# A PEER decoder trunk on one core: the low-part products of a dense tile go last, and the second products alternate between two halves

## The chip, the core and the metric

The kernel runs on one core of one Trainium2 chip. The metric is device time in microseconds (us). Three runs of the kernel before took 3287.05, 3287.91 and 3290.01 us, a median of 3287.91.

## What is computed

The reference is a decoder trunk of two layers on 512 tokens of width 1024. Layer 0 mixes tokens by retention, layer 1 by differential attention. Each is followed by a layer norm, a PEER feed-forward block and another layer norm. The change lies in the PEER block, where each token picks 128 of 16384 experts:

```python
def peer_ffn(x, w_q, subkeys, u, v):
    ...
        top, pos = lax.top_k(cand, PEER_TOPK)
        idx = jnp.take_along_axis(cidx, pos, axis=-1).reshape(PEER_CHUNK, PEER_HEADS * PEER_TOPK)
        gate = jax.nn.softmax(top, axis=-1).reshape(PEER_CHUNK, PEER_HEADS * PEER_TOPK)
        u_e = jnp.take(u, idx, axis=0)
        v_e = jnp.take(v, idx, axis=0)
        act = jax.nn.gelu(jnp.einsum('ted,td->te', u_e, xc).astype(jnp.float32))
        return jnp.einsum('te,ted->td', (gate * act).astype(v_e.dtype), v_e)
```

## The kernel before

Products of float32 matrices are made of three products. Each operand is split into a high part, rounded by ScalarE (`split`, line 103), and a low part, the rest, by VectorE or GpSimd (line 104). `mm3` (line 106) adds high x high, high x low and low x high into one PSUM bank. `wload` brings a 512 KB block of weights into one of nine raw buffers and splits it into `wh` and `wl`, which have three buffers each.

The first 128 tokens take the sparse way: their experts' rows are gathered one by one (`sparse_u`, `sparse_v`), a VectorE instruction for each. The other 384 tokens (`DT`) take the dense way: for all 16384 experts, 128 at a time, the activation is computed, multiplied by a gate that is zero for experts not picked, and used in a second product.

- A **dense tile** (`u_tile`, line 869) is the first product of 128 experts with 384 tokens: 8 blocks `k` of the width, three products of 128x384 each, 24 in all, into a bank `mu` or `rt`; ScalarE's gelu takes the result to `uact`.
- A **second-product step** (`v_mm`, line 888, called for 3 token tiles `t`) multiplies the gated activations (`wwh`, `wwl`, made by `v_prep`) with 128 rows of v, in two halves `c` of 512 columns: 18 products of 128x512 into six accumulators, four banks `pj` and two `rt`, which stay open over all 128 steps.

Names in a profile's rows are "out<-moving,stationary": `mu<-xth,wh` is high x high, `mu<-xtl,wh` the low part of x with the high part of the weights, `mu<-xth,wl` the product that needs `wl`. In the second products `wwh` and `wwl` are the stationary operand.

`peer` runs in two parts per layer. In the **first part** top-k, one-hot gates (`gates`, `gmat`) and sparse dot products run on VectorE, while TensorE makes the first 82 dense tiles ahead and stores them (`ad`). In the **second part** the 128 steps run; the stored tiles are read back for the first 82, after which dense tiles and steps take turns, with four tiles ahead (`LEAD`). The main line of that loop is

```python
preps.append(v_prep(kp, l, a, act, g[:, :, a % GA, :]))
if a < P - NB:
    for t in range(DT // P):
        v_mm(preps[0], t, acc)
```

Each engine runs its instructions in a fixed order. That order is made when the program is built, by a scheduler that places instructions by their operands' readiness in its own timeline; so an edit to the order of products can move instructions on other engines.

Of the kernel before, what the change touches and what calls it, by code (L numbers as in the profile page):

```python
# [29 lines left out]
P = 128  # L30
S = 512
D = 1024
TB = S // P
KD = D // P
# [10 lines left out]
DT = 384  # L45
# [18 lines left out]
def build(tc, I, out):  # L64
    nc = tc.nc
    ctx = ExitStack()
    with ctx:
# [18 lines left out]
        XTH = xp.tile([P, KD, S], F32R, name="xth")  # L86
        XTL = xp.tile([P, KD, S], F32R, name="xtl")

        def bank(tag):
            return psum.tile([P, 512], F32, name=tag, tag=tag, bufs=4 if tag == "pj" else 2)  # L90


        newest = {}
# [12 lines left out]
        def mm3(o, ah, al, bh, bl, start, stop):  # L106
            nc.tensor.matmul(o, ah, bh, start=start, stop=False)  # L107
            nc.tensor.matmul(o, ah, bl, start=False, stop=False)  # L108
            return nc.tensor.matmul(o, al, bh, start=False, stop=stop)  # L109

        def wload(src, eng=None, pool=None, tag="", bufs=3, dst=None):
            a = src.shape[1]
            pool = pool or wp
            raw = wp.tile([P, 1024], F32, name="wraw", tag="wraw", bufs=RING)
            nc.sync.dma_start(raw.rearrange("p (a b) -> p a b", a=a), src)
            if dst is None:
                h = pool.tile([P, 1024], F32R, name="wh", tag="wh" + tag, bufs=bufs)
                l = pool.tile([P, 1024], F32R, name="wl", tag="wl" + tag, bufs=bufs)
            else:
                h, l = dst  # L120
            split(h, l, raw, eng)
            return h.rearrange("p (a b) -> p a b", a=a), l.rearrange("p (a b) -> p a b", a=a)
# [746 lines left out]
        def u_tile(dp, l, a, tag="mu"):  # L869
            uh, ul = wload(I[f"ut{l}"][a])  # L870
            b = bank(tag)
            for k in range(KD):
                newest["mm"] = mm3(b[:, :DT], uh[:, k, :], ul[:, k, :], XTH[:, k, S - DT:], XTL[:, k, S - DT:], k == 0, k == KD - 1)
            act = dp.tile([P, DT], F32, name="uact", tag="uact", bufs=LEAD + 1)
            newest["gelu"] = nc.scalar.activation(act, b[:, :DT], AF.Gelu_apprx_tanh)
            return act
# [11 lines left out]
        def v_mm(prep, t, acc):  # L888
            a, (vh, vl), wh, wl = prep
            ts = slice(t * P, t * P + P)  # L890
            for c in range(2):
                mm3(acc[t][c], wh[:, ts], wl[:, ts], vh[:, c, :], vl[:, c, :], a == 0, a == P - 1)

        def peer(l, norm, feed, prepare):
            with tc.tile_pool(name="sp", bufs=1, reuse_waits="tile") as sp, tc.tile_pool(name="dp", bufs=1, reuse_waits="tile") as dp:
# [6 lines left out]
                with tc.tile_pool(name="p1", bufs=1, reuse_waits="tile") as kp:  # L902
# [10 lines left out]
                    with tc.tile_pool(name="tk", bufs=1, reuse_waits="tile") as tp:  # L913
# [43 lines left out]
                        for cost in gates():  # L957
                            tv += cost
                            while tu < tv and nu < P:
                                act = u_tile(dp, l, nu, ("mu", "rt")[nu % 2])  # L960
                                nc.sync.dma_start(ad[nu], act)
                                nu += 1
                                tu += UT
                                while nd < DOTS * (nu - LAG):
                                    with behind("low"):
                                        next(su, None)
                                    nd += 1
                                    tv += 1.2
                with tc.tile_pool(name="p2", bufs=1, reuse_waits="tile") as kp:
# [18 lines left out]
                    def u_ahead():  # L988
                        nonlocal used
                        while len(ahead) < LEAD and nu + used < P:  # L990
                            ahead.append(u_tile(dp, l, nu + used))
                            used += 1
# [3 lines left out]
                    for a in range(P):  # L996
                        if a < GA * NG0:
                            g = G0[a // GA]
                        elif a % GA == 0:
                            g = dp.tile([P, DT // GT, GA, GT], F32, name="gl", tag="gl", bufs=2)  # L1000
                            nc.sync.dma_start(g.rearrange("p q a t -> p (q a t)"),
                                              gd.rearrange("g p q f -> g p (q f)")[a // GA - NG0])
                        if a < nu:
                            act = kp.tile([P, DT], F32, name="aact", tag="aact", bufs=4)
                            nc.sync.dma_start(act, ad[a])
                        else:
                            act = ahead.pop(0)
                            u_ahead()
                        due += (flow * time[a] - load[a]) / row
# [4 lines that stand above are left out]
                            preps.pop()  # L1014
                        while done < due:
                            next(su2, None)
                            done += 1
# [5 lines left out]
                    for t in range(DT // P):  # L1023
                        for p in preps:
                            v_mm(p, t, acc)
                        if t and norm.dst is None:
                            norm.tr()
                        for c in range(2):
                            half_sum(acc[t][c], t + 1, c, True)
                        norm.ln(t + 1)  # L1030
# [74 lines left out]
```

## Time and profile before

| what | value |
|---|---|
| median of three runs | 3287.91 us |
| the profiled execution, its own time | 3291.58 us |
| its span, first to last instruction | 3289.8 us |
| mean granted TensorE clock | 0.989 of full speed |
| HBM traffic | 692.88 MB read, 78.38 MB written |

PE is TensorE's matmuls, PEld its weight loads, DVE is VectorE, ACT ScalarE, POOL GpSimd, SP the engine that issues most transfers. The page tells shares of the whole span. A table by windows gives each engine's busy time in a stretch with the granted clock, a list of waits gives who stood still for whom, and a timeline gives single instructions with, in brackets, the idle time before one and what ended it. Two matmul records overlap, as a matmul's row lasts past the next one's start; the step from start to start is the pace.

### The profile page before, as it was taken

How to read it: one execution, taken by the hardware profiler on the slowest of the kernel's cores; microseconds unless marked ns; L12 is line 12 of the kernel's file. 1: busy time of each engine (PE TensorE's matmuls, PEld its weight loads, DVE VectorE, ACT ScalarE, POOL GpSimd, SP SyncE). 2: the span in 40 equal slices, each digit the busy share in tenths (PEclk: the TensorE clock that was granted, in tenths of full speed). 3: DMA queues.
4: the chain of work that ended last, by engine and by line, in shares of the span. 5: the costliest groups of instructions: out<-in, count | busy, mean ns of one | idle time of the engine just before them, and what ended most of it. 6: DMA issues, size and time to landing. Idle time of an engine off the chain costs nothing.

```text
span 3289.8 us, 47157 instructions
## 1 busy us (share of the span) xinstructions
PE 3202.7 (97%) x16666; PEld 2844.6 (86%) x16666; DVE 2520.6 (77%) x4849; ACT 1397.4 (42%) x2436; POOL 1020.3 (31%) x663
## 2 busy tenths in 40 slices
PE   9999999899999999999999999989999999999998
PEld 7888889899998888889888668989999788888987
DVE  4444468999868888888863564899987888888886
ACT  3323333367763333333333652335777333333332
POOL 1101330211113333455424423125531233345540
PEclk9999999999999999999999999999999999999999
DMA  5222223577789999899943212347787999999993
GB/s 212 87 84 87 90 91 123 186 237 250 254 271 347 359 353 351 331 350 356 345 151 102 71 34 80 122 166 240 251 260 256 350 354 366 341 334 349 354 339 135
DMA packets 310078, 774.39 MB, mean 235 GB/s; under 512 B 25936, under 2 KB 154320, under 8 KB 306256
## 3 DMA queue, kind: packets, MB, share of 16 engines
q1 hardware_dynamic: 236112, 502.89, 43.5%
q0 software_dynamic: 73728, 268.47, 22.6%
q8 instruction: 131, 2.15, 0.3%
q14 instruction: 107, 0.88, 0.1%
HBM read 692.88 MB, written 78.38 MB: 234 GB/s over the span
## 4 chain that ended last, share of the span: by engine, by line
PE 60%; DVE 6%; issue 2%; ACT 1%; DMA 1%; POOL 0%; POOLq 0%; DVEq 0%; ACTq 0%
PE pj L107 9%; PE pj L108 9%; PE pj L109 9%; PE mu L109 5%; PE mu L107 5%; PE mu L108 5%; PE rt L108 5%; PE rt L107 5%; PE rt L109 5%; PE pj L844 2%; DVE wl L104 1%; PE mu L499 1%; DVE tk_idf L736 1%; DVE x L767 0%; PE rt L536 0%
## 5 line engine op out<-in xcount | busy, mean ns | idle before, releaser
L103 ACT ACTIVATE wh<-wraw 128x1024 fp32r<-128x1024 f32 x632 | 659.0, 1054 | 590.9 <-PE mu L108 119.6
L104 DVE TENSOR_TENSOR wl<-wraw,wh 128x1024 fp32r<-128x1024 f32 x572 | 699.2, 1232 | 202.1 <-ACT wh L103 193.9
L752 POOL DMA_INDIRECT ug<-in_u,idx x256 | 433.2, 1692 | 1155.9 <-DVE wl L104 577.6
L109 PE MATMUL mu<-xth,wl 128*128 128x384 f32 (+1 forms) x1424 | 481.5, 338 | 16.5 <-DVE wl L104 16.5
L107 PE MATMUL mu<-xth,wh 128*128 128x384 f32 (+1 forms) x1424 | 482.1, 339 | 9.8 <-ACT wh L103 7.3
L108 PE MATMUL mu<-xtl,wh 128*128 128x384 f32 (+1 forms) x1424 | 478.8, 336 | 0.0
L765 POOL DMA_INDIRECT vg<-in_v,idx x256 | 337.7, 1319 | 330.0 <-DVE x L767 233.0
L108 PE MATMUL pj<-wl,wwh 128*128 128x512 f32 x1024 | 400.6, 391 | 0.0
L103 ACT ACTIVATE wwh<-w 128x384 fp32r<-128x384 f32 x256 | 134.3, 526 | 625.6 <-issue 365.9
L109 PE MATMUL pj<-wh,wwl 128*128 128x512 f32 x1024 | 397.2, 389 | 0.0
L107 PE MATMUL pj<-wh,wwh 128*128 128x512 f32 x1024 | 382.5, 392 | 7.4 <-ACT wwh L103 7.4
L754 DVE CUSTOM_DVE_ANT_0 scr<-ug,x 128x1024 bf16<-128x1024 f32 x256 | 314.4, 1228 | 33.6 <-DMA ug<-in_u,idx 33.2
L767 DVE SCALAR_TENSOR_TENSOR x<-vg,wgt,x 128x1024 f32<-128x1024 f32 x256 | 328.5, 1283 | 3.9 <-DMA vg<-in_v,idx 0.4
L109 PEld LDWEIGHTS mu<-xth,wl 128*128 128x128 f32 x1424 | 270.2, 190 | 21.9 <-DVE wl L104 21.6
L107 PEld LDWEIGHTS mu<-xth,wh 128*128 128x128 f32 x1424 | 270.3, 190 | 16.4 <-ACT wh L103 9.6
L108 PEld LDWEIGHTS mu<-xtl,wh 128*128 128x128 f32 x1424 | 270.6, 190 | 3.6
L104 DVE TENSOR_TENSOR wwl<-w,wwh 128x384 fp32r<-128x384 f32 x256 | 143.0, 560 | 125.1 <-ACT wwh L103 112.6
L109 PE MATMUL rt<-xth,wl 128*128 128x384 f32 (+1 forms) x688 | 230.2, 335 | 7.2 <-DVE wl L104 7.2
L107 PE MATMUL rt<-xth,wh 128*128 128x384 f32 (+1 forms) x688 | 231.1, 336 | 0.2
L107 PEld LDWEIGHTS pj<-wh,wwh 128*128 128x128 f32 x1024 | 192.7, 189 | 44.5 <-ACT wwh L103 8.0
L108 PE MATMUL rt<-xtl,wh 128*128 128x384 f32 (+1 forms) x688 | 229.5, 334 | 0.5 <-DVE xtl L104 0.5
L109 PEld LDWEIGHTS pj<-wh,wwl 128*128 128x128 f32 x1024 | 192.3, 188 | 40.1
(242 smaller groups left out, 6316.2 us busy)
## 6 DMA issues: line engine op xcount, KB each, us to landing
wraw<-in_ut SPq DMA_DIRECT2D x256, 512.0 KB
wraw<-in_v SPq DMA_DIRECT2D x256, 512.0 KB
gd<-g_st SPq DMA_DIRECT2D x48, 896.0 KB
gl<-gd SPq DMA_DIRECT2D x28, 1536.0 KB
ad<-uact SPq DMA_DIRECT2D x164, 192.0 KB
aact<-ad SPq DMA_DIRECT2D x164, 192.0 KB
wraw<-in_w_in SPq DMA_DIRECT2D x48, 512.0 KB
wraw<-in_peer_w_q SPq DMA_DIRECT2D x32, 512.0 KB
```

Source lines behind the costliest of these rows:

```text
L103: nc.scalar.activation(h, src, AF.Copy)
L104: newest["low"] = (eng or nc.vector).tensor_tensor(out=l, in0=src, in1=h.bitcast(F32), op=OP.subtract)
L107: nc.tensor.matmul(o, ah, bh, start=start, stop=False)
L108: nc.tensor.matmul(o, ah, bl, start=False, stop=False)
L109: return nc.tensor.matmul(o, al, bh, start=False, stop=stop)
L499: nc.tensor.matmul(b[:, :n], qt[g][ms, h, qb * P:qb * P + P], kt[g][ms, h, :n], start=True, stop=True)
L736: nc.vector.reduce_sum(out=idf[:, hs, :], in_=ex.rearrange("p h c k -> p h k c"), axis=AX.X)
L752: nc.gpsimd.indirect_dma_start(out=u, out_offset=None, in_=I[f"u{l}"], in_offset=bass.IndirectOffsetOnAxis(ap=idx[:, j:j + 1], axis=0))
L754: nc.vector.tensor_tensor_reduce(out=scr, in0=u, in1=X[t], scale=1.0, scalar=0.0, op0=OP.mult, op1=OP.add, accum_out=act[:, j:j + 1])
L765: nc.gpsimd.indirect_dma_start(out=v, out_offset=None, in_=I[f"v{l}"], in_offset=bass.IndirectOffsetOnAxis(ap=idx[:, j:j + 1], axis=0))
L767: nc.vector.scalar_tensor_tensor(out=X[t], in0=v, scalar=w[:, j:j + 1], in1=X[t], op0=OP.mult, op1=OP.add)
L844: nc.tensor.matmul(b[:, i * P:i * P + P], oh[:, 1, i, :], oh[:, 0, i, :], start=True, stop=True)
```

## The change

In `u_tile` the 24 products come in another order: for each `k` the two with the high part `uh`, then for each `k` the one with the low part `ul`. In `v_mm` the loop over the kind of product is now the outer one and the loop over the two halves the inner one. The products and their operands are the same.

```diff
--- before.py
+++ after.py
@@ -869,8 +869,12 @@
         def u_tile(dp, l, a, tag="mu"):
             uh, ul = wload(I[f"ut{l}"][a])
             b = bank(tag)
+
             for k in range(KD):
-                newest["mm"] = mm3(b[:, :DT], uh[:, k, :], ul[:, k, :], XTH[:, k, S - DT:], XTL[:, k, S - DT:], k == 0, k == KD - 1)
+                nc.tensor.matmul(b[:, :DT], uh[:, k, :], XTH[:, k, S - DT:], start=k == 0, stop=False)
+                nc.tensor.matmul(b[:, :DT], uh[:, k, :], XTL[:, k, S - DT:], start=False, stop=False)
+            for k in range(KD):
+                newest["mm"] = nc.tensor.matmul(b[:, :DT], ul[:, k, :], XTH[:, k, S - DT:], start=False, stop=k == KD - 1)
             act = dp.tile([P, DT], F32, name="uact", tag="uact", bufs=LEAD + 1)
             newest["gelu"] = nc.scalar.activation(act, b[:, :DT], AF.Gelu_apprx_tanh)
             return act
@@ -888,8 +892,9 @@
         def v_mm(prep, t, acc):
             a, (vh, vl), wh, wl = prep
             ts = slice(t * P, t * P + P)
-            for c in range(2):
-                mm3(acc[t][c], wh[:, ts], wl[:, ts], vh[:, c, :], vl[:, c, :], a == 0, a == P - 1)
+            for i, (w, v) in enumerate(((wh, vh), (wh, vl), (wl, vh))):
+                for c in range(2):
+                    nc.tensor.matmul(acc[t][c], w[:, ts], v[:, c, :], start=a == 0 and i == 0, stop=a == P - 1 and i == 2)
 
         def peer(l, norm, feed, prepare):
             with tc.tile_pool(name="sp", bufs=1, reuse_waits="tile") as sp, tc.tile_pool(name="dp", bufs=1, reuse_waits="tile") as dp:
```

Since the scheduler sets the order, three places of the built program are shown before and now.

TensorE, first part of layer 0, tile `rt_4858` (`wh_4854`, `wl_4855`) and the next, before:

```order
L107 MATMUL rt_4858<-xth_81,wh_4854 128x384
L108 MATMUL rt_4858<-xtl_82,wh_4854 128x384
L107 MATMUL mu_4897<-xth_81,wh_4893 128x384
L108 MATMUL mu_4897<-xtl_82,wh_4893 128x384
L109 MATMUL rt_4858<-xth_81,wl_4855 128x384
L107 MATMUL rt_4858<-xth_81,wh_4854 128x384
L108 MATMUL rt_4858<-xtl_82,wh_4854 128x384
L109 MATMUL rt_4858<-xth_81,wl_4855 128x384
```

and now, the last products of the same tile:

```order
L875 MATMUL rt_4858<-xtl_82,wh_4854 128x384
L874 MATMUL rt_4858<-xth_81,wh_4854 128x384
L875 MATMUL rt_4858<-xtl_82,wh_4854 128x384
L877 MATMUL rt_4858<-xth_81,wl_4855 128x384 x8
L874 MATMUL mu_4897<-xth_81,wh_4893 128x384
L875 MATMUL mu_4897<-xtl_82,wh_4893 128x384
```

Before, the next tile's first two products stood between the second and the third of this one; now the tile's 24 products stand together, `wl` last.

TensorE at the turn to the second part of layer 0: the fourth tile ahead, `mu_9069`, and the first second-product step, before (four more products into `rt` follow, and then the other 22 of the tile):

```order
L107 MATMUL mu_9069<-xth_81,wh_9065 128x384
L108 MATMUL mu_9069<-xtl_82,wh_9065 128x384
L107 MATMUL pj_8953<-wh_9100,wwh_9106 128x512
L108 MATMUL pj_8953<-wl_9101,wwh_9106 128x512
L107 MATMUL pj_8954<-wh_9100,wwh_9106 128x512
L108 MATMUL pj_8954<-wl_9101,wwh_9106 128x512
L107 MATMUL pj_8955<-wh_9100,wwh_9106 128x512
L108 MATMUL pj_8955<-wl_9101,wwh_9106 128x512
```

and now:

```order
L875 MATMUL mu_9069<-xtl_82,wh_9065 128x384
L874 MATMUL mu_9069<-xth_81,wh_9065 128x384
L875 MATMUL mu_9069<-xtl_82,wh_9065 128x384
L877 MATMUL mu_9069<-xth_81,wl_9066 128x384 x8
L897 MATMUL pj_8953<-wh_9100,wwh_9106 128x512
L897 MATMUL pj_8954<-wh_9100,wwh_9106 128x512
L897 MATMUL pj_8953<-wl_9101,wwh_9106 128x512
L897 MATMUL pj_8954<-wl_9101,wwh_9106 128x512
```

The tile's 24 products now stand in front of the step. On VectorE these rows stand in the same order before and now (before is shown; `wl_9066` is this tile's low part, `wwh_9106` is made from `w_9104`):

```order
L104 TENSOR_TENSOR wl_9209<-wraw_9206,wh_9208 128x1024
L881 TENSOR_TENSOR w_9104<-aact_9096,gl_3194 128x384
L881 TENSOR_TENSOR w_9142<-aact_9134,gl_3194 128x384
L104 TENSOR_TENSOR wl_9066<-wraw_9063,wh_9065 128x1024
L754 ISA scr_5277,act0_3191<-ug_9341,x0_77 128x1024
L754 ISA act0_3191 128x1
L104 TENSOR_TENSOR wwl_9107<-w_9104,wwh_9106 128x384
```

What moved there is TensorE's order alone.

TensorE, the second step of layer 0, token tile 0 (`pj_8953` and `pj_8954` are its two halves), before:

```order
L107 MATMUL pj_8953<-wh_9138,wwh_9144 128x512
L108 MATMUL pj_8953<-wl_9139,wwh_9144 128x512
L109 MATMUL pj_8953<-wh_9138,wwl_9145 128x512
L107 MATMUL pj_8954<-wh_9138,wwh_9144 128x512
L108 MATMUL pj_8954<-wl_9139,wwh_9144 128x512
L109 MATMUL pj_8954<-wh_9138,wwl_9145 128x512
```

and now:

```order
L897 MATMUL pj_8953<-wh_9138,wwh_9144 128x512
L897 MATMUL pj_8954<-wh_9138,wwh_9144 128x512
L897 MATMUL pj_8953<-wl_9139,wwh_9144 128x512
L897 MATMUL pj_8954<-wl_9139,wwh_9144 128x512
L897 MATMUL pj_8953<-wh_9138,wwl_9145 128x512
L897 MATMUL pj_8954<-wh_9138,wwl_9145 128x512
```

The output bank now changes at each product, and the stationary operand once in these six rather than three times.

## Rows read from the trace of the kernel before

**Rows 1.** The page, part 1: engine, busy us (share of the span), instructions.
```profile
PE 3202.7 (97%) x16666; PEld 2844.6 (86%) x16666; DVE 2520.6 (77%) x4849; ACT 1397.4 (42%) x2436; POOL 1020.3 (31%) x663
```

**Rows 2.** The timeline, PE alone, products of a tile and of second-product steps.
```profile
589.45 0.33 PE L109 MATMUL mu<-xth,wl 128*128 128x384 f32 x1
589.63 0.33 PE L107 MATMUL mu<-xth,wh 128*128 128x384 f32 x1
...
2799.67 0.39 PE L107 MATMUL pj<-wh,wwh 128*128 128x512 f32 x1
2799.89 0.39 PE L108 MATMUL pj<-wl,wwh 128*128 128x512 f32 x1
2800.12 0.39 PE L109 MATMUL pj<-wh,wwl 128*128 128x512 f32 x1
2800.35 0.39 PE L107 MATMUL pj<-wh,wwh 128*128 128x512 f32 x1
```

**Rows 3.** Windows: us, busy us by engine (instructions), PE clock, DMA share, GB/s.
```profile
521.00:762.00 241.00, 230.23 (x1395) 227.01 (x1393) 236.14 (x685) 120.23 (x217) 39.62 (x20) 0.99 0.60 198
...
979.00:1000.00 21.00, 16.14 (x69) 14.32 (x70) 15.00 (x23) 4.82 (x11) 5.67 (x4) 0.84 0.96 345
1000.00:1290.00 290.00, 290.00 (x1281) 240.23 (x1280) 239.93 (x359) 104.05 (x142) 89.95 (x76) 1.00 0.95 357
1290.00:1710.00 420.00, 414.37 (x2043) 371.39 (x2043) 354.92 (x376) 143.56 (x198) 187.83 (x138) 0.99 0.86 317
```

**Rows 4.** Waits: us, times, longest; PE: whole span, last stages 1290 on, 2860 on; DVE 1300:1650.
```profile
PE mu L109 <- DVE wl L104: 16.5, 14, 3.4
...
PE rt L109 <- DVE wl L104: 7.2, 4, 2.1
...
PE mu L109 <- DVE wl L104: 3.0, 4, 1.4
...
PE mu L109 <- DVE wl L104: 2.6, 3, 1.4
...
DVE w L881 <- ACT uact L875: 23.4, 20, 3.8
```

**Rows 5.** Timeline, PE, one wait; windows (columns as rows 3) after waits.
```profile
649.62 0.54 PE L109 MATMUL mu<-xth,wl 128*128 128x384 f32 x1 [2.69 <-DVE wl L104]
...
649.80:653.20 3.40, 3.40 (x12) 3.40 (x13) 3.40 (x16) 0.00 (x0) 0.94 (x1) 0.50 1.01 372
...
987.70:994.50 6.80, 5.84 (x14) 4.69 (x15) 4.87 (x8) 1.37 (x3) 2.83 (x2) 0.50 0.95 319
1434.90:1438.30 3.40, 3.40 (x13) 3.40 (x12) 3.33 (x4) 0.00 (x0) 1.49 (x2) 0.50 0.86 283
1571.40:1574.80 3.40, 3.40 (x11) 3.40 (x12) 3.37 (x3) 0.00 (x0) 2.62 (x2) 0.50 0.82 233
```

**Rows 6.** The timeline, ACT alone, first part of layer 0.
```profile
595.00 1.06 ACT L103 ACTIVATE wh<-wraw 128x1024 fp32r<-128x1024 f32 x1 [2.87 <-PE rt L108]
```

**Rows 7.** Timeline of PE, then DVE, then the chain, the turn of layer 0.
```profile
984.17 0.33 PE L107 MATMUL mu<-xth,wh 128*128 128x384 f32 x1
...
988.66 0.79 PE L107 MATMUL pj<-wh,wwh 128*128 128x512 f32 x1 [3.97 <-ACT wwh L103]
...
988.43 1.22 DVE L104 TENSOR_TENSOR wl<-wraw,wh 128x1024 fp32r<-128x1024 f32 x1
...
998.24 0.93 PE pj L109 x4
```

**Rows 8.** The timeline, PE alone, last stage of layer 0.
```profile
1431.86 0.44 PE L107 MATMUL mu<-xth,wh 128*128 128x384 f32 x1 [1.33 <-ACT wh L103]
...
1433.84 0.44 PE L109 MATMUL mu<-xth,wl 128*128 128x384 f32 x1 [1.37 <-DVE wl L104]
```

**Rows 9.** The timeline, PE alone, four products in a row to four banks, twice.
```profile
1293.22 1.07 PE L107 MATMUL pj<-wh,wwh 128*128 128x512 f32 x4
...
1367.33 1.09 PE L107 MATMUL pj<-wh,wwh 128*128 128x512 f32 x4
```

## The prediction

> **What bounds the kernel now.** I read the page's shares first, then the table by stage, then TensorE's waits, then single stretches. The page puts the PE at 97% of the span, with DVE second at 77% [rows 1]. A PE busy record is longer than the step to the next one, so the pace is read from starts: a 128x512 product of `v_mm` starts 0.22 to 0.23 us after the one before, and a 128x384 product of `u_tile` 0.17 to 0.18 us after [rows 2]. At 0.227 and 0.173 us the 24 products of a dense tile take 4.15 us, and the 18 of one second-product step 4.09 us. Where nothing is late, as in the stage from 1000 to 1290 us, PE is busy throughout at a granted clock of 1.00 [rows 3]. So the number and shape of matmuls set most of the time, and this change alters neither. What it can move is the time in which PE stands still or runs at half clock.
>
> The table by stage has three kinds of such places, each once per layer. In the first part of a layer's PEER (521 to 762 us: dense tiles beside the top-k) PE misses 11 us, while DVE is busy 236.14 of 241 us; in the turn from the first part to the second (979 to 1000) PE is busy 16.14 of 21 us at a mean clock of 0.84; in the last stage (1290 to 1710: dense tile and second products in turn) it misses 5.6 us [rows 3]. The waits name what is late: of all PE waits the largest two groups are a product with the weights' low part, L109, for DVE's `wl`: 16.5 us in 14 waits and 7.2 us in 4 [rows 4]. Some are paid twice: after the 2.69 us wait that ends at 649.62 the granted clock is 0.50 for the next 3.40 us, and so it is at 1434.9, 1571.4 and, for 6.80 us, at 987.7 [rows 5]. Half clock for 3.4 us costs 1.7 us of product time.
>
> **The change part by part.** Edit 1, dense tiles (256 of them): the first product with `wl` moves from place 3 to place 17, that is 14 x 0.173 = 2.4 us later after the tile's start. The high part is now last used at place 16, not 23, so its buffer comes free 7 x 0.173 = 1.2 us earlier; ScalarE's next `wh` waits for just that release [rows 6]. `wl` takes DVE 1.22 us [rows 7], so a `wl` that comes straight after its `wh` is in time. The count of products stays. No DMA is added, and SP's and POOL's queues keep their work. I cost this edit at each place.
>
> (a) The last stage. At 1431.86 PE waits 1.33 us for `wh`, does two products, waits 1.37 us for `wl`, and then runs at half clock from 1434.9 [rows 5, 8]. With the new order the 1.37 us lie behind 14 further products. The stage's `wl` waits are 3.0 us in layer 0 and 2.6 us in layer 1 [rows 4], and each has two stretches at half clock (1434.9 and 1571.4 in layer 0), worth 3.4 us. Bounds: nothing, if the loads or DVE pace the stage, and 6.4 and 6.0 us. DVE is busy 354.92 of 420 us and from 1300 to 1650 waits 23.4 us itself for the gelu of PE's tiles [rows 3, 4]: it follows PE and has room. So I take the waits whole and one half-clock stretch of two, as the 1.33 us wait for `wh` stays: 4.7 + 4.3 = 9.0 us.
>
> (b) The turn. In the order before, the fourth tile ahead issues two products at 984.17, then twelve second products that wait until 988.66 for `wwh`; they run at half clock, and the tile ends at 998.24 [rows 7]. In the new order the tile's 16 high products come at once, done by 984.17 + 2.77 = 986.94. Its `wl` is DVE's row at 988.43, done 989.65, and DVE's order there is unchanged. So a new wait of 2.7 us stands where 3.97 us stood, with eight products after it (1.38 us, to 991.03) and then the same twelve (2.72 us, to 993.75). Against 998.24 that is 4.5 us less. But an idle time of 2.69 us was followed by 3.4 us at half clock [rows 5], so I take 1.7 us off: 2.8 us a layer, 5.6 in all; bounds 1.1 (6.8 us at half clock, as now) and 4.5.
>
> (c) The first part. Here DVE is nearly full, and what it does before a tile's `wl` isn't shortened by PE's order. A stage paced by DVE gives back the shift just once, 2.4 us. It also has a cost: up to the 30th one-hot block the new DVE order pulls at most three instructions of `wl`'s size ahead, 3 x 1.22 = 3.7 us. The upper bound is every wait for `wl` outside the last stages, (16.5 + 7.2 - 3.0 - 2.6)/2 = 9.0 us a layer [rows 4], and the half-clock stretch at 649.8, 1.7 us: 10.7. The nearest row is the DVE's 236.14 of 241, so I take the low value, 2.4 us a layer, 4.8 in all; bounds -3.7 and 10.7.
>
> Edit 2, second products (256 steps of 18): three kinds alternate between the two halves, so the output bank changes at each product rather than at every third, and the stationary operand changes 6 times in 18 rather than 12. Into 2799.89 neither changes, into 2800.12 the stationary operand does, into 2800.35 both do: the steps are 0.22, 0.23 and 0.23 us [rows 2]. I take 0. Where four products in a row go to four banks already, their joint record is 1.07 us, or 1.09 us [rows 9]; three steps of 0.227 and one record of 0.39 [rows 2] make 1.07. So the bounds are 0 and 0.02/3, 6.7 ns a product, 31 us for 4608. The Trainium skill, in "TensorE: Matmul & The Clock Gate", Back-to-back issue gap, gives N/2.4 + 2.5 ns for an isolated gap, 216 ns here against our 227. If those 11 ns were the swap of the stationary operand, 6 x 256 swaps fewer would save an estimated 17 us, and the sum would be 3252; the equal steps with and without a swap speak against it.
>
> At the very end the last product of half 0 stands one step before the last of half 1 instead of three, so DVE may add that half two steps, 0.45 us, later. I count 0.5 us once.
>
> **Sum:** 9.0 + 5.6 + 4.8 - 0.5 = 18.9 us off. Of the profiled execution (3291.58 us, span 3289.8) that leaves 3272.7; against the median of the runs, 3287.91, which is 3.7 us shorter, it is 3269. The forecast's own range is 3255 to 3281: from (a) and (b) whole with half of (c), 12.4 + 9.0 + 11 = 32 us, to the least that shows. About 0.2% (6.6 us) is what a measurement here can tell from no change: faster is below 3281.3, slower above 3294.5.
>
> **Rivals.** First, paced elsewhere: (a) meets loads that come no earlier, the DMA share being 0.95 in the stage before [rows 3], and (c) only hands PE a longer wait for DVE. Then the waits change their name, from L109 for `wl` to the first product for `wh` or `g_oh`, and (b) at its lower bound and little else remain: some 4 us, 3284. For it: DVE's 236 of 241. Against: the 23.4 us in which DVE waits for PE.
>
> Second, more than I count: all bounds at their best, 12.4 + 9.0 + 21.4 = 43 us, 3245. For it: the earlier release of `wh` helps ScalarE start the chain that DVE ends. Against: DVE's share.
>
> Third, slower: the change of bank at each product costs 6.7 ns for all 4608 second products, 31 us, as the longer record in [rows 9] would have it. The slower stage gives the loads time, so (a) falls away, and 3287.9 + 31 - 9.9 = 3309. It decides from (9.9 + 6.6)/4608 = 3.6 ns a product on. Against: the shorter record, the step with a bank change at 0.23 us, and a stage that keeps clock 1.00 [rows 2, 3]. The Trainium skill warns, in "TensorE: Matmul & The Clock Gate", A second HAM failure mode: psum-queue depth-cycling, that cycling through banks can leave PE idle in small pieces and bring the low clock back; the 1.00 of the stage, which changes bank six times a step, does not agree.
>
> Fourth, the change does nothing that shows: 3288. The program's order speaks against it, since 14 products move ahead of each `wl`.
>
> **How the numbers follow.** Forecast 0.58; paced elsewhere 0.19; more than counted 0.10; slower by banks 0.10; nothing 0.03. The predicted time is the forecast's, 3269. The range 3248 to 3289 takes in the forecast's bounds, the first and fourth rivals and nearly all of the second. Faster is the forecast and the second: 0.68; same is the first and the fourth: 0.22; slower is the third: 0.10.
>
> **What would show it.** L877's waits for `wl` nearly gone in the last stage, a wait of some 2.7 us for `wl` at the turn in place of the 3.97 us for `wwh`, fewer stretches at clock 0.50 after 1290; in the first part DVE still near full with PE waiting now for `wl`, `wh` or `g_oh`. The step of second products must stay at 4.09 us: above 4.15 us the third rival holds. I am wrong if waits for `wh` or `g_oh` grow by what L877 loses.

## The result and the profile after

The changed kernel takes 3267.93 us (median of six runs, 3260.32 to 3271.54), the kernel before 3290.61 (six runs, the three known before among them): a ratio of 0.993, 95% interval 0.992 to 0.994, or 22.7 us less. Forecast were 3269 and 18.9 us less. Run once more beside the experiments, it took 3266.1 against 3292.13, ratio 0.992 (0.991 to 0.993). Its profiled execution took 3268.82 us with a span of 3267.1, against 3291.58 and 3289.8 before: 22.7 us there too. One run of e2 below, 8382.35 us at a granted clock of 0.533, is left out of its ratio.

The page, part 1, of the changed kernel (engine, busy us, share, instructions):

```profile
PE 3195.5 (98%) x16666; PEld 2841.6 (87%) x16666; DVE 2517.9 (77%) x4849; ACT 1413.9 (43%) x2436; POOL 934.2 (29%) x663
```

The counts of instructions are those of [rows 1]; DVE's work is the same, and PE is busy 7.2 us less in all. The windows of [rows 3], of the changed kernel:

```profile
521.00:762.00 241.00, 232.24 (x1416) 230.28 (x1415) 236.62 (x686) 124.63 (x218) 38.66 (x20) 0.99 0.61 201
979.00:1000.00 21.00, 18.90 (x85) 16.38 (x84) 19.58 (x32) 5.70 (x10) 7.69 (x6) 0.92 0.93 329
1000.00:1290.00 290.00, 290.00 (x1281) 240.23 (x1280) 242.08 (x359) 106.54 (x141) 91.19 (x76) 1.00 0.95 358
1290.00:1710.00 420.00, 416.45 (x2076) 373.04 (x2075) 354.65 (x384) 146.85 (x201) 184.18 (x138) 1.00 0.85 315
```

All three disturbed places of [rows 3] have gained: in the same microseconds PE gets through 21, 16 and 33 instructions more. (The windows are fixed in time and the changed kernel runs ahead, so they show that something was gained, not how much; the table below goes by work done.) In the first part DVE is as full as before (236.62 of 241 us). In the stage without dense tiles PE's row is the same, 1281 products in 290.00 us, although edit 2 has changed their order.

The waits of PE, of the whole span (us, times, longest):

```profile
PE mu L877 <- DVE wl L104: 15.1, 6, 5.2
...
PE mu L874 <- ACT wh L103: 6.6, 6, 1.1
PE rt L877 <- DVE wl L104: 5.6, 4, 1.5
```

and of the last stage of layer 0, from 1280 to 1705 us:

```profile
PE mu L874 <- ACT wh L103: 3.3, 3, 1.1
PE mu L877 <- DVE wl L104: 0.2, 1, 0.2
```

The waits for `wl` have not gone: 20.7 us in 10 waits stand where [rows 4] has 23.7 in 18. They have been gathered. In the last stage 3.0 us have shrunk to 0.2; in the first part of layer 0 five, the longest of 2.7 us, have become three, the longest of 5.2, and at the turn there is a new one. PE's timeline of the first part shows the long one:

```profile
644.31 0.34 PE L875 MATMUL mu<-xtl,wh 128*128 128x384 f32 x1
649.85 2.93 PE L877 MATMUL mu<-xth,wl 128*128 128x384 f32 x8 [5.20 <-DVE wl L104]
```

The turn of layer 0, PE's timeline, to set beside [rows 7]:

```profile
975.95 0.45 PE L874 MATMUL mu<-xth,wh 128*128 128x384 f32 x1 [0.43 <-ACT uact L879]
...
982.83 0.34 PE L875 MATMUL mu<-xtl,wh 128*128 128x384 f32 x1
985.26 2.66 PE L877 MATMUL mu<-xth,wl 128*128 128x384 f32 x8 [2.10 <-DVE wl L104]
987.72 1.06 PE L897 MATMUL pj<-wh,wwh 128*128 128x512 f32 x2
```

As foretold, the fourth tile's 16 high products run at once, and one wait for `wl`, 2.10 us, stands where 3.97 us for `wwh` stood; the tile is whole before the second products begin. The windows of the changed kernel in which the clock is at issue (columns as in [rows 3]):

```profile
985.60:989.00 3.40, 3.40 (x12) 3.12 (x10) 3.40 (x8) 0.06 (x1) 1.85 (x2) 0.50 1.02 365
...
2547.00:2557.00 10.00, 9.89 (x45) 8.45 (x46) 8.40 (x18) 2.79 (x6) 2.69 (x2) 1.00 1.01 384
...
1423.80:1430.00 6.20, 5.95 (x31) 5.37 (x31) 6.13 (x6) 3.16 (x4) 4.51 (x3) 1.00 0.64 190
1559.80:1566.00 6.20, 6.15 (x33) 5.82 (x34) 6.13 (x6) 2.61 (x4) 3.55 (x3) 1.00 0.72 223
...
647.70:654.50 6.80, 4.65 (x15) 4.65 (x16) 6.80 (x30) 1.06 (x1) 3.78 (x2) 0.50 0.71 255
```

The two places of the last stage that [rows 5] shows at 0.50 come 8 to 10 us earlier in the changed kernel, behind its waits for `wh` at 1423.8 and 1559.8, and there the clock is 1.00. The turn of layer 0 has 3.4 us at 0.50 instead of 6.8. The turn of layer 1 (the window from 2547) has none, although its wait for `wl` is as long:

```profile
2547.11 0.62 PE L877 MATMUL mu<-xth,wl 128*128 128x384 f32 x2 [2.11 <-DVE wl L104]
```

The first part of layer 0 has 6.8 us at 0.50 round its long wait; PE works for 4.65 us of them.

**Where the 22.7 us lie.** The table is worked out from the starts of PE's products in each trace. The first part of a layer's PEER runs from the first product of dense tile 0 to that of tile 82; the turn from there to step 6 of the second products (counted from 0); the second products alone until the next dense tile; the last stage to the last second product. Each column is the sum of both layers, in us; "rest" is the retention, the attention stage and the tail.

| profiled execution | first part | turn | second products alone | last stage | rest | span |
|---|---|---|---|---|---|---|
| before | 896.2 | 98.6 | 620.2 | 750.3 | 924.5 | 3289.8 |
| the change | 889.5 | 90.1 | 620.2 | 739.5 | 927.9 | 3267.1 |
| the change again | 890.0 | 87.5 | 620.2 | 739.4 | 926.5 | 3263.5 |

First part -6.7, turn -8.5, last stage -10.8: 26.0 us. The rest takes 3.4 us more; that is nearly all the attention stage (387.8 us before, 391.2 now; 389.6 in the second execution), which the change does not touch.

### The profile page after: what moved, and what is told of

Read it like the earlier page. It is cut to its first block, busy times and chain, and to the rows that moved or that the text cites. A ratio compares the mean times of both kernels' runs of the same rounds, so it can differ in the third digit from the quotient of the medians.

```text
span 3267.1 us, 47174 instructions
## 1 busy us (share of the span) xinstructions
PE 3195.5 (98%) x16666; PEld 2841.6 (87%) x16666; DVE 2517.9 (77%) x4849; ACT 1413.9 (43%) x2436; POOL 934.2 (29%) x663
## 3 DMA queue, kind: packets, MB, share of 16 engines
q0 software_dynamic: 73728, 268.47, 22.7%
## 5 line engine op out<-in xcount | busy, mean ns | idle before, releaser
L752 POOL DMA_INDIRECT ug<-in_u,idx x256 | 350.8, 1370 | 1222.6 <-DVE wl L104 633.4
L874 PE MATMUL mu<-xth,wh 128*128 128x384 f32 x1392 | 471.2, 339 | 7.5 <-ACT wh L103 6.6
L875 PE MATMUL mu<-xtl,wh 128*128 128x384 f32 x1392 | 468.8, 337 | 0.0
L897 PE MATMUL pj<-wl,wwh 128*128 128x512 f32 x1024 | 315.5, 390 | 0.0
L897 PE MATMUL pj<-wh,wwl 128*128 128x512 f32 x1024 | 315.0, 389 | 0.0
L897 PE MATMUL pj<-wh,wwh 128*128 128x512 f32 x1024 | 308.6, 391 | 0.0
L877 PE MATMUL mu<-xth,wl 128*128 128x384 f32 x1392 | 276.4, 339 | 15.1 <-DVE wl L104 15.1
L897 PEld LDWEIGHTS pj<-wl,wwh 128*128 128x128 f32 x1024 | 192.6, 188 | 40.7
L874 PE MATMUL rt<-xth,wh 128*128 128x384 f32 x656 | 221.3, 337 | 0.0
L875 PE MATMUL rt<-xtl,wh 128*128 128x384 f32 x656 | 220.0, 335 | 0.0
```

The source lines that it names most:

```text
L752: nc.gpsimd.indirect_dma_start(out=u, out_offset=None, in_=I[f"u{l}"], in_offset=bass.IndirectOffsetOnAxis(ap=idx[:, j:j + 1], axis=0))
L874: nc.tensor.matmul(b[:, :DT], uh[:, k, :], XTH[:, k, S - DT:], start=k == 0, stop=False)
L875: nc.tensor.matmul(b[:, :DT], uh[:, k, :], XTL[:, k, S - DT:], start=False, stop=False)
L877: newest["mm"] = nc.tensor.matmul(b[:, :DT], ul[:, k, :], XTH[:, k, S - DT:], start=False, stop=k == KD - 1)
L897: nc.tensor.matmul(acc[t][c], w[:, ts], v[:, c, :], start=a == 0 and i == 0, stop=a == P - 1 and i == 2)
```

## Experiments

Each was timed beside the kernel before on the same chip. Medians in us, ratio with its 95% interval, then the columns of the table above.

| kernel | median | before | ratio | first part | turn | alone | last | rest |
|---|---|---|---|---|---|---|---|---|
| e1 edit 1 alone | 3263.97 | 3291.56 | 0.992 (0.991 to 0.993) | 889.6 | 89.4 | 620.2 | 740.8 | 923.0 |
| e2 edit 2 alone | 3291.15 | 3291.56 | 1.000 (0.999 to 1.001) | 896.6 | 98.9 | 620.2 | 751.3 | 925.6 |
| e3 edit 1, second part | 3275.0 | 3291.56 | 0.995 (0.994 to 0.997) | 896.7 | 90.9 | 620.2 | 740.8 | 925.7 |
| e4 edit 1, first part | 3285.14 | 3291.56 | 0.998 (0.997 to 0.999) | 889.9 | 96.7 | 620.2 | 752.9 | 925.3 |
| e5 more swaps | 3268.36 | 3292.13 | 0.993 (0.992 to 0.994) | 889.9 | 86.2 | 620.2 | 741.1 | 928.8 |
| e6 the change again | 3266.1 | 3292.13 | 0.992 (0.991 to 0.993) | 890.0 | 87.5 | 620.2 | 739.4 | 926.5 |
| e9 cover, no release | 3268.4 | 3291.06 | 0.993 (0.992 to 0.995) | 892.3 | 84.0 | 620.2 | 744.8 | 925.4 |
| e11 four ahead | 3273.91 | 3291.08 | 0.995 (0.993 to 0.996) | 892.5 | 87.3 | 620.2 | 747.3 | 925.1 |
| e7 e1, later dots | 3259.14 | 3292.13 | 0.990 (0.989 to 0.992) | 879.0 | 99.2 | 628.3 | 726.3 | 924.5 |
| e8 both edits, later dots | 3259.68 | 3292.13 | 0.990 (0.989 to 0.992) | 881.1 | 104.5 | 628.3 | 724.5 | 925.5 |
| e10 e7, wwh behind wh | 3247.03 | 3291.06 | 0.987 (0.985 to 0.988) | 879.2 | 103.5 | 628.3 | 713.7 | 924.3 |

In e7, e8 and e10 the first part makes 83 dense tiles instead of 82. By the table's cuts that puts a tile (4.15 us a layer) into the turn and a step (4.09) into "alone", and takes both from the last stage; there only the sums of the three are to be compared.

### One edit at a time: e1 and e2

e1 has `u_tile` as changed and `v_mm` as before; e2 the other way round:

```diff
 def v_mm(prep, t, acc):
-    for c in range(2):
-        mm3(acc[t][c], wh[:, ts], wl[:, ts], vh[:, c, :], vl[:, c, :], a == 0, a == P - 1)
+    for i, (w, v) in enumerate(((wh, vh), (wh, vl), (wl, vh))):
+        for c in range(2):
+            nc.tensor.matmul(acc[t][c], w[:, ts], v[:, c, :], start=a == 0 and i == 0, stop=a == P - 1 and i == 2)
```

> Edit 1 alone: the dense tiles issue the eight products with the low part last; the second products stay as before (three products into a bank, then the other half). Theory (edit 1 brings the whole gain, alternating the banks is free): 3268 us, between 3264 and 3272, as the kernel with both edits. Rival A (the alternation earns a part, through fewer swaps of the stationary operand, 17 us at 11 ns each): 3278 to 3286. Rival B (the alternation costs something that edit 1 has covered up): 3260 or less.

> Edit 2 alone: dense tiles as before, kinds of second products alternating between the halves. Theory: no change, 3290 us, between 3286 and 3294, and 18 products in 4.09 us in the stage with second products alone. Rival A (fewer swaps of the stationary operand earn 17 us): 3273. Rival B (a change of bank at each product costs up to 6.7 ns): 3300 to 3321.

e2 came out at no change, as the theory had it, and e1 with the whole gain, 27.6 us. That is some 4 us more than theory, at the edge of what it allowed and towards its rival B. But rival B would need a place where the alternation costs something, and the table has none: e1 and the change differ by 0.7 us at the turn, by 1.3 in the last stage in the change's favour, and by 4.9 us in the rest. Run once more (e6), the change has e1's ratio, 0.992.

### The change again, and more swaps: e6 and e5

e5 is e1 with the three products of a bank in the order high-high, low-high, high-low, so that the stationary operand (`wh` or `wl`) changes more often:

```diff
-        mm3(acc[t][c], wh[:, ts], wl[:, ts], vh[:, c, :], vl[:, c, :], a == 0, a == P - 1)
+        o = acc[t][c]
+        nc.tensor.matmul(o, wh[:, ts], vh[:, c, :], start=a == 0, stop=False)
+        nc.tensor.matmul(o, wl[:, ts], vh[:, c, :], start=False, stop=False)
+        nc.tensor.matmul(o, wh[:, ts], vl[:, c, :], start=False, stop=a == P - 1)
```

> The change itself once more, beside the others of this chip. Theory (edit 2 does nothing; the 4 us by which edit 1 alone came out faster lie in the attention stage, which differs from run to run): ratio to the kernel before 0.992 to 0.993, 3264 to 3268 us. Rival (with edit 1 in place the alternation costs some 4 us): 3268 us or more, with a profile in which the turn or the last stage takes longer than with edit 1 alone (45.2 and 44.2, 370.8 and 370.0 us).

> Edit 1, and second products in which the stationary operand changes at each of a step's 18 products (three per bank in a row, as before, where it changed at 12; with the alternation it changes at 6). It prices the swap alone. Theory (a swap of the stationary operand is free): as edit 1 alone, 3264 us, between 3260 and 3268, and the stage with second products alone at 310.1 us. Rival (a swap costs 11 ns, the difference of our 227 ns a product to an estimate of 216): 6 x 256 x 11 ns = 17 us more, 3281.

e6's ratio is the theory's, and its turn (43.5 and 43.9 us) and last stages (370.2 and 369.3) are as short as e1's (45.2, 44.2; 370.8, 370.0), so rival B is out: the alternation costs nothing beside edit 1 either. For e5 the expectation miscounts: the last product of a bank and the first of the next half share their operand, so the swaps are 15 of 18 and the rival's price is 3 x 256 x 11 ns = 8.4 us, 3272. The median is 0.4 us above the theory's range, but not where a swap could cost: the stage with second products alone is the same 620.2 us, and in the profiled execution the surplus sits in the attention stage (392.6 us, 386.1 in e1). The windows of the stage with second products alone show it best; before, then e2, then e5:

```profile
1020.00:1290.00 270.00, 270.00 (x1193) 223.65 (x1192) 223.95 (x334) 97.30 (x133) 85.03 (x72) 1.00 0.95 357
```

```profile
1020.00:1290.00 270.00, 270.00 (x1193) 223.64 (x1192) 224.41 (x335) 98.89 (x131) 84.68 (x71) 1.00 0.95 357
```

```profile
1020.00:1290.00 270.00, 270.00 (x1193) 223.65 (x1192) 225.85 (x342) 97.47 (x132) 84.90 (x73) 1.00 0.97 361
```

1193 products in 270 us, 226.3 ns each, whether the stationary operand changes at 12, 6 or 15 products of a step, and whether the bank changes at 6 or at all 18.

### Which stage: e3 and e4

A flag in `u_tile` chooses the order by its caller: e3 has the new order in `u_ahead`'s tiles alone, e4 in those of the loop over `gates()`.

```diff
-def u_tile(dp, l, a, tag="mu"):
+def u_tile(dp, l, a, tag="mu", second=True):
...
-            act = u_tile(dp, l, nu, ("mu", "rt")[nu % 2])
+            act = u_tile(dp, l, nu, ("mu", "rt")[nu % 2], False)
```

> The new order in the dense tiles of the second part of PEER alone (the turn and the last stage), the old one in the first part; second products as before. Theory (turn and last stage carry most of it: by the excess over PE's own pace some 4 us at the turn and 5.5 in the last stage of each layer, 19 us): 3271 us, between 3267 and 3276, with L109's waits for wl back in the first part. Rival (the turn's gain depends on where the first part leaves DVE and ScalarE, so the first part carries half): 3278 to 3282.

> The new order in the dense tiles of the first part alone (those made beside the top-k), the old one at the turn and in the last stage; second products as before. Theory (DVE paces the first part, so only 1 to 3 us a layer come off): 3286 us, between 3283 and 3289, with the last stages' waits for wl (3.0 and 2.6 us) and their four stretches at half clock as before. Rival (first part carries half): 3278 to 3282. Rival (a longer wait for wl elsewhere in the first part gives it back): 3290 or above.

Both as the theory had it: 16.6 us off for the second part, 6.4 for the first. The columns separate: e3 has the short turn and last stage with the old first part, e4 the reverse. Together they make 23.0 us of e1's 27.6; by the stages of the table, the rest left out, 22.3 of 25.3. Whether the other 3 us need both or are the difference between two executions is not shown. Of the four stretches at half clock that I expected in e4's last stages three are there. The waits of the last stage (1320 to 1700) for e3, then e4:

```profile
PE mu L874 <- ACT wh L103: 4.0, 3, 1.3
PE mu L877 <- DVE wl L104: 0.2, 1, 0.2
```

```profile
PE mu L107 <- ACT wh L103: 4.0, 3, 1.3
PE mu L109 <- DVE wl L104: 3.2, 4, 1.4
```

The same three waits for `wh`; those for `wl` only with the old order.

### Cover or release: e9 and e11

Edit 1 does two things to a tile: 14 products are put ahead of the first with `wl`, and the high part's buffer comes free 7 products sooner. e9 keeps the first and not the second: the last pair of high products stands behind the low ones (the diff is against the new order).

```diff
-for k in range(KD):
+for k in range(KD - 1):
     nc.tensor.matmul(b[:, :DT], uh[:, k, :], XTH[:, k, S - DT:], start=k == 0, stop=False)
     nc.tensor.matmul(b[:, :DT], uh[:, k, :], XTL[:, k, S - DT:], start=False, stop=False)
 for k in range(KD):
-    newest["mm"] = nc.tensor.matmul(b[:, :DT], ul[:, k, :], XTH[:, k, S - DT:], start=False, stop=k == KD - 1)
+    nc.tensor.matmul(b[:, :DT], ul[:, k, :], XTH[:, k, S - DT:], start=False, stop=False)
+nc.tensor.matmul(b[:, :DT], uh[:, KD - 1, :], XTH[:, KD - 1, S - DT:], start=False, stop=False)
+newest["mm"] = nc.tensor.matmul(b[:, :DT], uh[:, KD - 1, :], XTL[:, KD - 1, S - DT:], start=False, stop=True)
```

> A dense tile issues seven of its eight pairs of high products, then the eight with the low part, then the last pair: the first product with wl is 2.1 us later than before (2.4 with edit 1), but the high part is held to the tile's end as before. Second products as before. Theory (what counts is the work put between a tile's start and its first product with wl): nearly all of edit 1's gain, 3266 us, between 3263 and 3271, last stages of 371 and 370 us, turns of 45 to 46. Rival (what counts is the buffer of the high part, free 1.2 us sooner, so that ScalarE starts the next one earlier): last stages of 374 us or more, 3278 to 3286.

The total held: 22.7 us off, the turn the shortest of all. The last stages, 372.9 and 372.0 us, lie between the theory's 371 and 370 and the rival's 374. That is 2.0 us a layer more than in e1, and the waits of layer 0 (1320 to 1700) show most of it:

```profile
PE mu L873 <- ACT wh L103: 5.3, 4, 1.3
PE mu L876 <- DVE wl L104: 0.6, 1, 0.6
```

one more wait for `wh` than e1's three, with 0.4 us more for `wl`. e9 releases later and also covers two products less, and these runs do not separate the two. The first part is 1.3 us a layer longer than e1's, the turn 2.7 shorter. In sum the four columns make 2341.3 us against e1's 2340.0, and by the medians 22.7 us are off against 27.6: the cover is most of the gain, the release at most a fifth.

e11 is a small dose, without the long pile of low products at the end:

```diff
-for k in range(KD):
+for k in range(KD + 2):
+    if k < KD:
         nc.tensor.matmul(b[:, :DT], uh[:, k, :], XTH[:, k, S - DT:], start=k == 0, stop=False)
         nc.tensor.matmul(b[:, :DT], uh[:, k, :], XTL[:, k, S - DT:], start=False, stop=False)
-for k in range(KD):
-    newest["mm"] = nc.tensor.matmul(b[:, :DT], ul[:, k, :], XTH[:, k, S - DT:], start=False, stop=k == KD - 1)
+    if k >= 2:
+        newest["mm"] = nc.tensor.matmul(b[:, :DT], ul[:, k - 2, :], XTH[:, k - 2, S - DT:], start=False, stop=k == KD + 1)
```

> A smaller dose of edit 1: the low product of each k stands behind the two high products of k + 2, so that the first product with wl is at place 7 of a dense tile, four products or 0.69 us later than before, where edit 1 makes it 2.4 us. Second products as before. Theory (each wait shrinks by the work put ahead of it, and no further): of the last stage's waits for wl, 0.58, 1.37, 0.37 and 0.65 us, only 0.68 us of the second is left, so that stage comes to 372 to 374 us (before 375.9, edit 1 370.8); the waits of the turn and of the first part, up to 4 us, are hardly covered: 1 to 2 us off each. All in all 3279 us, between 3275 and 3283. Rival (it is the place at the end that counts, and what it makes of the order on the other engines): a last stage of 375 us or more and 3286 or above.

In the last stage (374.3 and 373.0 us) the waits did shrink by about the work put ahead (1320 to 1700):

```profile
PE mu L874 <- ACT wh L103: 4.0, 3, 1.3
PE mu L877 <- DVE wl L104: 1.7, 2, 1.1
```

3.0 us in four waits became 1.7 in two, not the one of 0.68 that I had worked out; why is not shown. The total was a miss, 1 us below the range. I had 1 to 2 us off each turn, and it was 5.6 on the mean, as much as edit 1 gets there (4.6 in e1, 5.6 in e6), with less than a third of its shift. In layer 0's turn PE's waits are 1.1 us for `wwh` and 0.9 for `uact`, where they were 4.0 and 1.2, and the clock stays at 1.00 from 984 to 1012:

```profile
984.00:1012.00 28.00, 27.91 (x127) 23.66 (x128) 24.96 (x39) 9.87 (x17) 7.96 (x8) 1.00 0.97 365
```

The two waits are 3.2 us shorter, and the 6.8 us at half clock, of which PE worked 5.84 [rows 5], cost 2.9 us more. So at the turn the clock behind a wait counts for about as much as the wait's own length.

### What paces the first part: e7 and e8

e7 is e1 with the sparse products on VectorE started later and taken more densely, their number by the end of the first part the same:

```diff
-DOTS = 0.6
-LAG = 22
+DOTS = 0.86
+LAG = 40
```

> Edit 1 alone, and the sparse products on VectorE start at the 40th dense tile instead of the 22nd, more of them per tile (0.86 for 0.6), so that their count by the end of the first part is the same: some 11 of 1.3 us leave the stretch from 560 to 700 us, in which VectorE never waits, for the stretch from 860 to 960, in which it waits 24 us. Theory (VectorE paces the first part, and PE's 5.2 us wait for wl with the half-clock stretch behind it is VectorE's backlog): 8 to 10 us a layer, 3245 us, between 3242 and 3252. Rival (the wait comes from the order at that place, a row of long reductions ahead of wl, not from the backlog): 3262 to 3266. Rival (the backlog only moves behind 760 us): 3258 to 3266 with new waits there.

> The same later start of the sparse products with both edits. Theory (edit 2 free): the same time as edit 1 with the later start, within 3 us. Rival (the alternation costs 4 us): 4 us more than that.

e8's median equals e7's, so edit 2 is free here as well (its profiled execution, 3265.72 us, is the longest of four, with 4.5 us for `wl` in layer 0's turn, and its stages are no comparison). e7 is a miss: 4.8 us less than e1 where I expected 16 to 20. In the first part it gains 5.3 us a layer, but 1.7 of them are given back behind the turn (turn, alone and last together 1453.8 us against 1450.4). The time lies in the range of the second rival, 3258 to 3266, and a little of it is there: four waits of 1.33 us for `wh` in each last stage instead of three. The waits of the first part (521 to 960), e1 and then e7:

```profile
PE mu L877 <- DVE wl L104: 5.2, 1, 5.2
PE rt L877 <- DVE wl L104: 2.9, 2, 1.5
PE rt L820 <- DVE g_if L817: 1.0, 1, 1.0
PE pj L844 <- DVE g_oh L840: 0.8, 1, 0.8
```

```profile
PE mu L877 <- DVE wl L104: 3.0, 1, 3.0
PE rt L877 <- DVE wl L104: 2.4, 2, 1.5
```

and the windows of the stretch of the long wait, e1 and then e7:

```profile
620.00:660.00 40.00, 32.40 (x173) 31.04 (x172) 40.00 (x103) 12.74 (x15) 8.78 (x6) 0.91 0.64 217
```

```profile
620.00:660.00 40.00, 36.12 (x198) 35.22 (x198) 40.00 (x154) 16.50 (x21) 0.00 (x0) 0.96 0.52 158
```

DVE is busy 40 of 40 us in both. With every sparse product gone from this stretch 3.0 of the 5.2 us remain: so the backlog of sparse products explains 2.2 of them. The rest is probably VectorE's other work there, top-k among it, or its order; that was not tried by itself.

### The waits that edit 1 leaves in the last stage: e10

ScalarE and PE of the changed kernel at one of the remaining waits:

```profile
1418.65 0.49 ACT L879 ACTIVATE uact<-mu 128x384 f32<-128x384 f32 x1 [4.12 <-PE mu L877]
1422.30 0.52 ACT L103 ACTIVATE wwh<-w 128x384 fp32r<-128x384 f32 x1 [3.16 <-PE rt L897]
1422.73 1.99 ACT L103 ACTIVATE wh<-wraw 128x1024 fp32r<-128x1024 f32 x2
```

```profile
1423.82 0.44 PE L874 MATMUL mu<-xth,wh 128*128 128x384 f32 x1 [1.11 <-ACT wh L103]
```

Here, and again at 1492.1 and 1559.8, once in eight tiles, `wwh` stands ahead of both `wh` on ScalarE and waits for the end of a second-product step; the `wh` behind it comes too late for PE. e10 is e7 (in which there are four such waits a layer) with `wwh` queued behind the newest dense tile's `wh`; `behind` orders an instruction after another, here both of the split:

```diff
-nc.scalar.activation(h, src, AF.Copy)
+newest["high"] = nc.scalar.activation(h, src, AF.Copy)
...
 uh, ul = wload(I[f"ut{l}"][a])
+newest["uh"] = newest["high"]
...
-split(wh, wl, w)
+with behind("uh"):
+    split(wh, wl, w)
```

> Edit 1 with the later start of the sparse products, and on ScalarE each wwh (the high part of a second product's weights) queued behind the wh of the newest dense tile. In the last stage PE's 1.33 us waits for wh come once in eight tiles, where ScalarE's order has wwh, which waits for a step's end, ahead of both wh. Theory (that order makes these waits): the waits go, 4 x 1.5 us a layer, 12 us, and 3247 us, between 3244 and 3252. Rival (wh is then in time but wwh late, and PE waits for that): 3256 to 3264. Rival (the loads are late in these places, the DMA share being 0.9): no change, 3259.

The theory's number: 3247.03 us, 12.1 less than e7. By the stages 6.3 us come off each last stage, and each turn takes 2.1 us more: its wait for `wl` is 3.7 us there, against 2.6 and 2.4 in e7. (The profiled execution, 3250.87 us, is the longest of four.) ScalarE of e10 at the same point of a tile no longer waits at `wwh`:

```profile
1412.53 0.49 ACT L880 ACTIVATE uact<-mu 128x384 f32<-128x384 f32 x1 [5.50 <-PE mu L878]
1412.92 1.05 ACT L103 ACTIVATE wh<-wraw 128x1024 fp32r<-128x1024 f32 x1
1413.87 0.51 ACT L103 ACTIVATE wwh<-w 128x384 fp32r<-128x384 f32 x1
```

and PE has no wait left in the stage; windows of e7, then e10:

```profile
1330.00:1680.00 350.00, 344.66 (x1734) 312.09 (x1733) 295.32 (x295) 122.47 (x166) 166.16 (x120) 1.00 0.91 335
```

```profile
1330.00:1680.00 350.00, 350.00 (x1765) 317.74 (x1764) 303.68 (x307) 121.84 (x172) 161.06 (x120) 1.00 0.90 332
```

e10 beats both kernels: 1.3% under the kernel before.

## Why the prediction was right, term by term

That the time came within 1.1 us of 3269 is in part luck. The three gains were each forecast too small, 19.4 us in sum where the profiles have 26.0; the attention stage, which the change leaves alone, took 3.4 us of that back; and the kernel before has a median 2.7 us above the one from which 3269 was reckoned.

**The last stage (forecast 9.0, measured 10.8).** The mechanism is the one given: the waits for `wl` fell from 3.0 to 0.2 us with the time of DVE's work unchanged (354.65 us against 354.92), and e3 against e4 shows that it is the order of these tiles. Mis-sized was the half clock: I kept one stretch of two, "as the 1.33 us wait for `wh` stays". Waits for `wh` stay, even three of 1.11 us (3.3) for two of 1.33, which in layer 0 were

```profile
PE mu L107 <- ACT wh L103: 2.7, 2, 1.3
```

and yet both stretches have gone. In layer 0: 2.8 off the waits for `wl`, 3.4 for two stretches, less 0.6 for `wh`, makes 5.6; measured 5.7. In e1 and e3 a wait of 1.33 us alone left the clock at 1.00; in the kernel before, the same wait was followed two products later by a second one of 1.37 us.

**The turn (forecast 5.6, measured 8.5 and 11.1).** The new wait is 2.10 us where I worked out 2.7. I left out the tile before: its wait for `uact` is 0.43 us now, and before it was

```profile
979.89 0.44 PE L107 MATMUL mu<-xth,wh 128*128 128x384 f32 x1 [1.25 <-ACT uact L875]
```

And the clock: I charged 3.4 us of half clock behind the new wait in each layer. In the profiled execution they are there in layer 0 and not in layer 1. In the second one there are none in either, with waits of 1.36 and 1.78 us; its window over the turn of layer 0:

```profile
976.00:1012.00 36.00, 34.21 (x162) 29.35 (x161) 31.07 (x48) 11.98 (x21) 10.67 (x9) 1.00 1.00 372
```

My bound of 4.5 us a layer already had the stretch spared whole. The 6.2 us of this turn exceed it by what I had left out or too long: 0.8 us of the wait for `uact`, and a wait for `wl` of 1.36 us for 2.7. (The twelve second products ahead of the tile's other 22 are as the prediction counts them; the text at the order rows, with six shown and four more, misses the two of the fourth `pj` bank.)

**The first part (forecast 4.8, measured 6.7).** DVE is nearly full there, as forecast (236.62 of 241 us busy, and never idle from 560 to 700 us in e1), and the order of size was right. But no row shows the term itself, a shift of 2.4 us given back just once; that it came near is luck. PE's listed waits between 521 and 962 us fell from 11.3 us to 9.3 in layer 0, which is 2.0 of the 3.7 us gained there. Another 1.1 us is the clock: before, PE worked through two stretches at 0.50, that of [rows 5] from 649.8 and this one,

```profile
629.30:632.70 3.40, 3.40 (x13) 3.40 (x12) 3.40 (x5) 0.00 (x0) 3.40 (x1) 0.50 0.09 14
```

6.8 us in all; now it works 4.65 us at 0.50. In layer 1 the waits fell by 4.3 us, while the clock took back 2.9, for this stretch at 0.50 is new there:

```profile
2211.00:2217.80 6.80, 5.81 (x18) 5.81 (x19) 6.80 (x29) 1.06 (x1) 2.91 (x2) 0.50 0.81 261
```

Of the 3.0 us gained in layer 1 1.6 stay open, and 0.6 in layer 0. The wait of 5.2 us that took the place of several shorter ones is of the kind that the forecast named as a sign, PE waiting for `wl` there; by e7 the sparse products make 2.2 us of it. (Of all PE waits the prediction called the 7.2 us of `rt` the second largest group; they are fifth, behind 7.4 us for `wwh` at the turns and two groups of 7.3 for `wh`.)

**Edit 2 (forecast 0, measured 0).** e2, e6 against e1, and e8 against e7 agree, and the third rival, 6.7 ns for a change of bank, is out: 226.3 ns a product with 6 changes a step or 18. The longer joint records of [rows 9] were no price. The Trainium skill's "TensorE: Matmul & The Clock Gate", Back-to-back issue gap, gives 216 ns at this width for an isolated gap. This trace has 226.3, and e5 shows that the difference is not the swap of the stationary operand, which an estimate from that figure priced at 17 us. The Trainium skill's warning on the same page, under A second HAM failure mode: psum-queue depth-cycling, is of small idle times between groups of products that cycle through banks, and of a clock that falls with them. Here neither shows: in a stage that changes bank at every product PE is busy 290.00 of 290 us and the granted clock is 1.00.

**The tail (forecast +0.5).** With edit 2 it is 14.6 us in all its profiled executions, without it 14.8 to 15.2: 0.2 to 0.6 us shorter. The sign was wrong and the size of no account.

The other rivals: "paced elsewhere" named a true thing, the waits that change their name, but in the last stage only 0.6 us of them came; "more than counted", 43 us, would have needed the first part's waits gone, and DVE did not allow that.

## What to carry to other kernels

Where a tile's operand comes in two pieces from two engines in a row, put all products with the first piece ahead of those with the second. It adds no work, and where the engine that makes the second piece has room, as in the last stage here, the waits shrink by about the work put ahead of them; where that engine is full, as in the first part, they are mostly gathered into fewer and longer ones. Count what a wait drags behind it as well: in the last stage and at the turn, stretches at half clock were worth about as much as the waits themselves. When the waits on one engine are gone, look at what stands at the head of the next engine's queue: one instruction in eight tiles that waited for PE, ahead of two that were urgent, cost 12 us in all.

## What was not expected

Two profiled executions of one and the same kernel differ by 2.3 us in the turn of layer 0 (45.8 and 43.5 us): a wait of 2.10 us with 3.4 us at half clock behind it in one, of 1.36 us with none in the other. The length of the wait does not decide it alone. In the first execution layer 1 has 2.11 us and no half clock behind them, and e1 has a still longer one with none:

```profile
986.09 0.44 PE L877 MATMUL mu<-xth,wl 128*128 128x384 f32 x1 [3.06 <-DVE wl L104]
...
986.00:996.00 10.00, 9.91 (x45) 8.46 (x46) 8.80 (x18) 3.05 (x6) 2.76 (x3) 1.00 1.01 389
```

What does decide it stays open. And the attention stage, which no kernel here alters, took 386.1 to 392.6 us over these profiles. Differences of 3 or 4 us between two of the kernels therefore say nothing until the stages are set side by side.

A wait of 1.33 us by itself was never followed by half clock in e1's last stages, three times in each. In e11's, such a wait with a second of 1.05 us soon behind it was, in each layer; one with 0.66 us behind it was not.
